# Decay and factors of the delta rule by way of DRAM, and another estimate behind the order of its instructions

## The chip, the cores and the metric

The kernel runs on one core of one Trainium2 chip. The metric is the time of one execution in microseconds (us); the median of three runs is 2485.27 us. The core's engines work side by side, each in the order of its own queue: PE (matmuls, with the weight load PEld in front of each), DVE and ACT (elementwise work), POOL (slow elementwise work, here also the inversion of small triangular matrices) and SP, which issues all DMAs. An instruction that waits holds up all that stand behind it in its queue.

## The reference

One step of a four-layer model on 576 positions (512 of a new stream, 64 of a running one), 1024 channels, fp32. The mixers are pool, delta rule, attention, pool; each is followed by a conv feed-forward block. The part that changes is the delta rule (layer 1, 8 heads of 128 channels):

```python
qkv = silu(causal_conv(h @ w_in)); q, k, v = split(qkv)      # q and k are normalised per head
gc = cumsum(g, axis=-1)                                       # log of the decay, within a chunk
decay = exp(where(lower_incl, gc[:,None] - gc[None,:], -inf))
sol = triangular_solve(eye + (k*beta) @ k.T * decay_strict, [v*beta, k*beta*exp(gc)])
attn = (q @ k.T) * decay
qg = q * exp(gc);  kg = k * exp(gc[-1] - gc);  glast = exp(gc[-1])
for c in chunks:                                              # the recurrence
    v_new = u_c - w_c @ s
    o_c = qg_c @ s + attn_c @ v_new
    s = s * glast_c + kg_c.T @ v_new
o = rmsnorm(o, norm_w) * silu(z);  y = o @ w_out
```

## The kernel before

All matrix products with weights are done as three passes of rounded high and low parts, so TensorE is the engine with the most work. The delta rule's stage (`dn`) begins with 32 projections of 48 matmuls each (8 heads each of k, q, v and z), issued in the order of a list (`TN['order']`), and ends with the output projection, 8 times 48 matmuls. Between the projections' matmuls stands the work of the heads:

- `conv` (k, q, v): DVE scales the projection out of PSUM into a tile C, POOL clears C's head and copies three old columns into it (`G.memset(C[:,0:3])`, `G.tensor_copy(C[:,515:518])`), ACT multiplies C by the last tap, POOL copies six columns of C out as new state (`dn_so`), DVE adds three taps, ACT takes tanh and writes it over C, DVE makes the silu. ACT's multiply thus waits for POOL's two set-up instructions, and its tanh for POOL's copies out of C.
- `mat(h)`: k times k (10 matmul passes on PE), decay and scale; the matrix M goes to DRAM.
- `inverse(g)` for four heads at once: POOL inverts 72 blocks of 32x32 in 62 tensor_tensor instructions; the result goes to DRAM. Other POOL work is queued in between.
- `merge(h)`: loads the blocks (16 DMAs), joins them to the inverse U of 128 rows.
- `prep_rec(h)`: attn, kg, q times exp(gc). For exp(gc) `bank(h, None, ...)` spreads the head's row gc over 128 partitions with two matmuls, and ACT takes the exponential out of PSUM in two instructions.
- `rec(h)`: the recurrence over five chunks. At its end 640 factors r (the rmsnorm) are made on POOL with a power. Five fp32 matmuls (ten passes) spread them over 128 partitions, and DVE multiplies o out of PSUM in two instructions. `z_post` multiplies with the gate, and ACT and DVE make the high and low parts that the output projection reads.

The order of the whole program is made when it is built. `Flow` holds a clock for each engine (`clk`), charges every instruction a duration from a table (`cost`), and lets the task of highest priority whose inputs are ready by those clocks write its next instructions; projections have the lowest priority and fill what is left. Each engine's queue is then fixed in the order written. In `Flow.charge` an instruction of DVE and one of POOL never hinder each other. Pools of tiles are limited by class: `lim['M']` = 2 and `lim['U']` = 2. For a DMA the estimate has the charges

```python
self.clk["S"] = max(self.clk["S"], t, self.now) + 475
self.clk["D"] = max(self.clk["D"], self.clk["S"] + 650) + size / 360.0
end = self.clk["D"] + 900
```

Of the kernel before, what the change touches and what calls it, by code (L numbers as in the profile page):

```python
# [9 lines left out]
F32 = mybir.dt.float32  # L10
F32R = mybir.dt.float32r
BF16 = mybir.dt.bfloat16
AF = mybir.ActivationFunctionType
ALU = mybir.AluOpType
PSUM = bass.MemoryType.PSUM
# [21 lines left out]
class Flow:  # L37
# [61 lines left out]
    def cost(self, eng, op, out, ins, a, k):  # L99
        n = self.cols(out)  # L100
        ps = any(x.space == PSUM for x in ins) or out.space == PSUM
        if eng == "PE":
            if op == "transpose":
                return 216.0
            rhs = a[2] if len(a) > 2 else k["rhs"]
            st = out.ap[0][0]
            base = out.offset // st if st else 0
            pair, self.half = (self.half == (base - 64, n) and out.shape[0] <= 64), (base, n) if out.shape[0] <= 64 else None
            if pair and rhs.dtype == F32:
                return 45.0  # L110
            if rhs.dtype == F32:
                return 4 * max(n, 128) / 2.4 + 6
            if rhs.dtype == F32R:
                return max(n, 256) / 2.4 + 3
            return max(n, 128) / 2.4 + 3
        if eng == "V":
            ptr = 62.0 * sum(1 for x in ins if self.cols(x) == 1 and n > 1)
            if op == "reciprocal":
                return 60 + 6.3 * n
            if op in ("tensor_copy", "tensor_scalar", "memset") and not ps:  # L120
                return 68 + 0.52 * n + ptr
            return 68 + 1.042 * n + ptr
        if eng == "A":
            return (51 if ps else 94) + 0.833 * n + 93 * sum(isinstance(k.get(q), bass.AP) for q in ("bias", "scale"))
        if eng == "G":
            if k.get("op") == ALU.pow:
                return 225 * n
            if op == "tensor_tensor":
                return 149 + 2.1 * n
            if op == "tensor_copy":  # L130
                return 118 + 3.3 * n
            return (36 if op == "memset" else 161) + 0.83 * n
        return 50.0
    def charge(self, eng, op, a, k):
        args = [x for x in list(a) + list(k.values()) if isinstance(x, bass.AP)]
        if not args:
# [4 lines left out]
        for x in ins:  # L141
            w = self.when(x, eng)
            if w < self.INF:
                t = max(t, w)
        n = out.tensor.name
        if eng == "S":
            size = max(self.cols(x) * x.shape[0] for x in (out, *ins)) * 4
# [3 lines that stand above are left out]
        else:  # L151
            if eng == "A":
                fn = str(k.get("func", a[2] if len(a) > 2 else "")).split(".")[-1]
                if fn in self.TABLES and fn not in self.aset:
                    self.aset = self.TABLES[fn]
                    t += 1283
            if eng != "PE":
                t = max(t, self.la[n] if not self.wr.get(n) else 0)
            end = t + self.cost(eng, op, out, ins, a, k)
            self.clk[eng] = end  # L160
        self.lastend = end
        self.lastcost = (end - t, op, self.cols(out), out.shape[0], str(out.dtype).split('.')[-1], ','.join('%s%s%s' % ('p' if x.space == PSUM else 's', self.cols(x), str(x.dtype).split('.')[-1]) for x in ins), 'p' if out.space == PSUM else 's')
        lo, hi = self.span(out)
# [90 lines left out]
 'prep': 10,  # L254
 'rec': 2,
 'cv': 6,
 'M': 2,
 'tu': 4,
 'tu_': 2,
 'mg': 3,  # L260
 'U': 2,
 'v': 2,
 'vs': 2,
 'pr': 4,
# [7 lines left out]
 'pv': 4,  # L272
 'pz': 6,
 'w': 8,
 'order': 'k0 q0 q1 k1 k2 q2 k3 q3 v2 v0 v1 v3 k4 q4 k5 k6 q6 k7 q5 q7 z1 z0 z2 z3 v5 v4 v6 v7 z4 z5 z7 z6',
 'pa': 3,
 'pb': 2,
 'pc': 7,
# [11 lines left out]
class Step:  # L290
# [354 lines left out]
    def ffn(self,l,st,nst,gnext):  # L645
# [55 lines left out]
        def up(j,stag):  # L701
            def gen():
                if j==0:
                    f.lim["g"]=6
                    yield [("so",1)]
                    so[0]=self.s([128,4,NF],F32,"so",1)
                f.spawn(post(j),10)
# [473 lines left out]
    def dn(self,l,st,nst,gnext):  # L1181
# [7 lines left out]
        cst=c1([128,3],"cst"); mc=c1([128,1],"mc")  # L1189
        tok=c1([128,5,72],"tok")  # L1190
        bE=c1([128,5,8],"bE"); ngc=c1([128,5,8],"ngc"); beta=c1([128,5,8],"beta"); nbe=c1([128,5,8],"nbe"); ekg=c1([128,5,8],"ekg")
        gh=[None]
        cc=[slice(128*c,128*c+128) for c in range(4)]; sm=slice(512,576); ss=slice(SO,SO+64)
        blocks=[(128*b,128*b+128) for b in range(4)]+[(512,576)]
        def prep():
# [15 lines left out]
        def ab_post(P):  # L1211
# [29 lines left out]
            G.memset(g[:,:NT].bitcast(F32),0.0)  # L1241
            V.tensor_copy(g[0:8,:NT],F[0:8])
            V.tensor_tensor(out=g[32:40,:NT],in0=F[0:8],in1=g[0:8,:NT].bitcast(F32),op=ALU.subtract)
            f.free(Yt,t_)
            yield [F,("p",1)]
            p=self.p()
# [32 lines left out]
        def first(post):  # L1279
            def gen():  # L1280
                f.lim["w"]=TN['w']
                yield [f"{st}:abw"]
                wk,hk=yield from self.wget()
                wa,ha=abw[0]
                Wp=((wk,[None,None],128),(wa,[None,None],40))
                for h in (0,1):
                    for w,P,n in Wp:
                        yield [("p",1,"g")]
                        P[h]=self.p("g")
                        yield from self.gemm(P,w,0,self.xk,KD,halves=(h,),need=self.xneed(st),n=n)  # L1290
                f.free(*hk,ha)
                f.spawn(ab_post(Wp[1][1]),3)
                f.spawn(post(Wp[0][1]),6)
            self.job(gen,(W[:,:,1024:1152],KD,128))
# [76 lines left out]

        def mat(h):
            k=kq[h][:,0]
            yield [k[:,:579],("a",1,"M"),("p",2),("t",1)]
            M=self.a(cls="M"); r=self.s([128,5],F32,"t",8)
            p=self.p(); q=self.p()
            G.memset(r,1.0)
            for c in range(4): mm(p[:,cc[c]],k[:,cc[c]],k[:,cc[c]],start=True,stop=True)
# [125 lines left out]
        def prep_rec(h):  # L1504
# [3 lines left out]
            yield [("a",2,"pr"),("a",1,"eg"),("p",2),("d",1,"ks"),("t",1)]  # L1508
            at=self.a(cls="pr"); eg=self.a(cls="eg"); kg=self.a(cls="pr"); kgs=self.d("ks")[:64]; gl=self.s([128,5],F32,"t",8)
            p=self.p(); q=self.p()  # L1510
            bank(h,self.mneg,p,q,0)
            yield [p,q,"@A"]
            for c in range(4): A.activation(at[:,cc[c]],p[:,cc[c]],AF.Exp,bias=ngc[:,c,h:h+1])
# [4 lines left out]
            yield [p,q,"@V"]  # L1518
            V.tensor_tensor(out=at[:,:512],in0=p,in1=at[:,:512],op=ALU.mult)
            V.tensor_tensor(out=at[:64,sm],in0=q[:64,:64],in1=at[:64,sm],op=ALU.mult)  # L1520
            yield [at]
            bank(h,None,p,q,0)
            yield [p,q,"@A"]
            A.activation(eg[:,:512],p,AF.Exp)
            A.activation(eg[:,sm],q[:,:64],AF.Exp)
            yield [eg]
            for b in range(4): T_(p[:,cc[b]],k[:,cc[b]],self.ident)
            T_(q[:64,:128],k[:,ss],self.ident)
            G.tensor_copy(gl[:,0:4],eg[:,127:512:128]); G.tensor_copy(gl[:,4:5],eg[:,575:576])
# [9 lines left out]
        def rec(h):  # L1539
# [56 lines left out]
            sq=self.a(cls="eg")  # L1596
            A.activation(sq[:,:NT],o[:,:NT],AF.Square)
            q=yield from sums(sq,512)
            f.free(sq)
            yield [("t",1)]  # L1600
            r=self.s([128,5],F32,"t",8)
            V.scalar_tensor_tensor(out=r,in0=q[:,:5],scalar=1.0/128,in1=eq[:,h],op0=ALU.mult,op1=ALU.add)
            G.tensor_tensor(out=r,in0=r,in1=mhalf,op=ALU.pow)
            yield [r,("p",1)]
            p=self.p()
            for i in range(4): mm(p[:,cc[i]],r[:,i:i+1].to_broadcast([128,128]),self.ident,start=True,stop=True)
# [8 lines left out]
        def z_post(h):  # L1615
# [25 lines left out]
                dno[h]=t  # L1641
                f.fire(f"{st}:o{h}")
            return g
        f.lim.update({k:TN[k] for k in ('cv','M','tu','tu_','mg','U','v','vs','pr','eg','ks','o_','S','rr')})
        def k_(h):
            if h: proj(8+h,qk_post(h,0),TN['pk'])
            else: first(qk_post(0,0))
# [390 lines left out]
```

## Time and profile before

| | us |
|---|---|
| median of three runs (2484.01 to 2489.79) | 2485.27 |
| the profiled execution | 2487.87 |
| its span, first to last instruction | 2486.1 |
| PE busy / PEld busy | 2440.4 / 2381.6 |
| DVE / ACT / POOL busy | 1904.6 / 1282.5 / 373.1 |
| mean granted TensorE clock, share of 2.4 GHz | 0.995 |

In the span the pool layer lies up to 145 us, its feed-forward block up to 435, the delta rule from 435 to 872, then feed-forward, attention (about 1436 to 1603), feed-forward, pool and the last feed-forward. All work of the helper `Eng.call` stands under one line of the code, L26, so that instructions are told apart by the tiles that they write and read: `p` is PSUM, `a` and `b` are wide SBUF tiles, `h` the split weights, `xh` and `xl` the parts of the normed input, `d` a small tile or a DRAM tensor, `t` the small tiles with the 640 factors.

### The profile page before, as it was taken

What the parts mean: (1) busy time and instruction counts of PE and PEld (TensorE: products, weight loads), DVE (VectorE), ACT (ScalarE), POOL (GpSimd) and SP (SyncE); (2) the same over time, 40 slices, a digit from 0 to 9 for tenths busy, and PEclk for the clock granted to TensorE, in tenths of its full rate; (3) what the DMA queues carried; (4) which work ended last, traced back from release to release, by engine and by line L of the source; (5) the groups of instructions that cost most, each with busy time, mean ns of one, the idle gap of its engine ahead of it and who ended that gap; (6) DMA issues with size and microseconds to landing.
All of it is one profiled execution on the core that took longest, in us unless ns stands there. A gap on an engine that the chain in (4) does not pass through costs nothing.

```text
span 2486.1 us, 46793 instructions
## 1 busy us (share of the span) xinstructions
PE 2440.4 (98%) x18385; PEld 2381.6 (96%) x18385; DVE 1904.6 (77%) x3695; ACT 1282.5 (52%) x2419; POOL 373.1 (15%) x750
## 2 busy tenths in 40 slices
PE   8999999998999999999999999999999999999998
PEld 7999999998999999999999998899999999999998
DVE  6888877887556478877886777778777788977775
ACT  6445544544344344444556677644444466544445
POOL 0000000138431101000000322200000011100000
PEclk9999999999999999999999999999999999999999
DMA  4323323332321221323334122222223231323231
GB/s 111 88 86 102 95 80 97 103 96 62 82 64 50 86 87 52 103 85 94 94 109 128 49 88 65 92 77 78 85 87 101 85 111 49 91 76 94 86 102 57
DMA packets 349056, 212.92 MB, mean 86 GB/s; under 512 B 30298, under 2 KB 341210, under 8 KB 348836
## 3 DMA queue, kind: packets, MB, share of 16 engines
q1 hardware_dynamic: 348836, 209.93, 28.9%
q8 instruction: 145, 2.38, 0.4%
q14 instruction: 75, 0.61, 0.1%
HBM read 192.41 MB, written 17.47 MB: 84 GB/s over the span
## 4 chain that ended last, share of the span: by engine, by line
PE 88%; DVE 4%; issue 3%; POOL 3%; DMA 1%; ACT 1%; SPq 0%; DVEq 0%; POOLq 0%; ACTq 0%
PE p L26 88%; DVE a L26 2%; DVE h L26 1%; POOL h L26 1%; POOL q L26 1%; ACT a L26 1%; DMA b<-in_x_prompt_dram 0%; DVE r L26 0%; DVE b L26 0%; POOL a L26 0%; DMA a<-in_cache_sb_k_dram 0%; ACT b L26 0%; POOL t L26 0%; POOL dn_so L26 0%; SPq L26 0%
## 5 line engine op out<-in xcount | busy, mean ns | idle before, releaser
L26 PE MATMUL p<-xh,h 128*128 128x288 f32 x4992 | 1061.5, 300 | 4.6 <-DVE h L26 4.4
L26 PEld LDWEIGHTS p<-xh,h 128*128 128x128 f32 x4992 | 820.9, 189 | 10.1 <-DVE h L26 4.8
L26 PE MATMUL p<-xl,h 128*128 128x288 f32 x2496 | 720.3, 296 | 0.0
L26 ACT ACTIVATE h<-r 128x512 fp32r<-128x512 f32 (+1 forms) x688 | 499.6, 747 | 411.6 <-PE p L26 327.3
L26 PE MATMUL p<-b,h 128*128 128x288 f32 x4992 | 677.9, 296 | 4.9 <-DVE b L26 2.3
L26 PEld LDWEIGHTS p<-b,h 128*128 128x128 f32 x4992 | 666.2, 189 | 8.1 <-DVE b L26 3.8
L26 DVE TENSOR_TENSOR h<-r,h 128x512 fp32r<-128x512 f32 (+1 forms) x688 | 571.5, 840 | 43.3 <-ACT h L26 41.8
L26 PEld LDWEIGHTS p<-xl,h 128*128 128x128 f32 x2496 | 472.8, 189 | 0.5
L26 DVE TENSOR_TENSOR a<-p,a 128x288 f32<-128x288 f32 (+4 forms) x662 | 269.5, 446 | 204.9 <-PE p L26 190.7
L26 PE MATMUL p<-a,h 128*128 128x288 f32 x2448 | 347.6, 295 | 4.6 <-DVE h L26 3.9
L26 PEld LDWEIGHTS p<-a,h 128*128 128x128 f32 x2448 | 331.8, 188 | 6.3 <-DVE h L26 4.8
L26 POOL COPY so<-a 128x2 f32<-128x2 f32 x176 | 98.1, 587 | 1488.6 <-DVE a L26 1488.6
L26 ACT ACTIVATE a<-a 128x512 f32<-128x512 f32 (+7 forms) x358 | 192.4, 559 | 130.6 <-DVE a L26 109.9
L26 ACT ACTIVATE q<-p 128x288 f32<-128x288 f32 x272 | 111.6, 410 | 168.4 <-PE p L26 165.0
L26 DVE SCALAR_TENSOR_TENSOR a<-a,fcw,a 128x578 f32<-128x578 f32 x176 | 144.2, 819 | 6.8 <-ACT a L26 1.7
L26 ACT ACTIVATE b<-a 128x576 fp32r<-128x576 f32 x96 | 65.4, 682 | 87.4 <-DVE a L26 87.3
L26 ACT ACTIVATE xh<-a,gains 128x288 fp32r<-128x288 f32 (+2 forms) x128 | 66.3, 531 | 70.2 <-DVE a L26 69.7
L26 DVE TENSOR_TENSOR a<-p,q 128x288 f32<-128x288 f32 (+2 forms) x204 | 66.6, 355 | 46.5 <-PE p L26 46.5
L26 ACT ACTIVATE a<-p 128x448 f32<-128x448 f32 (+5 forms) x149 | 64.8, 454 | 71.7 <-PE p L26 54.4
L26 POOL TENSOR_TENSOR a<-a,a 128x512 fp32r<-128x512 f32 (+1 forms) x64 | 68.2, 1065 | 220.7 <-DVE a L26 202.4
L26 DVE TENSOR_TENSOR r<-r 128x512 f32<-128x512 f32 x136 | 94.4, 694 | 4.1
L26 PE MATMUL p<-a,a 128*128 128x128 f32 (+6 forms) x656 | 94.4, 284 | 1.1 <-ACT b L26 0.8
(192 smaller groups left out, 2457.2 us busy)
## 6 DMA issues: line engine op xcount, KB each, us to landing
r<-in_ffn_w_up_dram SPq DMA_DIRECT2D x176, 512.0 KB
r<-in_ffn_w_down_dram SPq DMA_DIRECT2D x80, 512.0 KB
r<-in_dn_w_in_dram SPq DMA_DIRECT2D x32, 512.0 KB
r<-in_sb_w_qkv_dram SPq DMA_DIRECT2D x24, 512.0 KB
d<-a SPq DMA_DIRECT2D x24, 288.0 KB
a<-d SPq DMA_DIRECT2D x16, 288.0 KB
r<-in_ffn_w_down_dram SPq DMA_DIRECT2D x16, 256.0 KB
r<-in_dn_w_out_dram SPq DMA_DIRECT2D x8, 512.0 KB
```

The costliest lines, as they stand in the source:

```text
L26: r = f(*a, **k)
```

## The change

It has five parts, all within the delta rule's stage.

1. exp(gc): once per stage ACT takes the exponential of the 8 rows and SP writes them to DRAM (`eD`, 8x576). In `prep_rec` a DMA reads the head's row into all 128 partitions of `eg`; the two matmuls of `bank(h,None)` and the two exponentials out of PSUM are gone.
2. The factors r of heads 0 to 6: SP writes the 640 values to DRAM (a store of single elements), waits, reads them back into 128 partitions of `sq`; DVE multiplies in one instruction from SBUF. Head 7 keeps the matmuls. The tile `sq`, of class `eg`, is held until that multiply.
3. `Flow` gets a third clock, "port": while `turns` is on, an instruction of POOL that reads SBUF, and one of DVE that reads two wide SBUF operands (or is a copy or tensor_scalar from SBUF), begin only when the last such instruction has ended. `first` of the delta rule turns it on, the first up-projection of the next feed-forward block off. The instructions of attention stand in the same order as before, row by row.
4. `M` takes its tiles from class `U`, whose limit is 4.
5. The list of projections is another.

```diff
+    turns = False
+    def port(self, eng, op, ins):
+        n = sum(1 for x in ins if x.space != PSUM and self.cols(x) > 1)
+        if eng == "G":
+            return n > 0
+        return eng == "V" and (n > 1 or n == 1 == len(ins) and op in ("tensor_copy", "tensor_scalar"))
...
+            port = self.turns and self.port(eng, op, ins)
+            if port:
+                t = max(t, self.clk["port"])
             end = t + self.cost(eng, op, out, ins, a, k)
             self.clk[eng] = end
+            if port:
+                self.clk["port"] = end
...
- 'M': 2,
- 'U': 2,
+ 'U': 4,
...
- 'order': 'k0 q0 q1 k1 k2 q2 k3 q3 v2 v0 v1 v3 k4 q4 k5 k6 q6 k7 q5 q7 z1 z0 z2 z3 v5 v4 v6 v7 z4 z5 z7 z6',
+ 'order': 'k0 k1 q0 q1 k2 k3 q2 q3 v0 v1 k4 k5 q4 k6 k7 q5 q6 q7 v2 v3 z0 z1 v4 v5 z2 z3 v6 v7 z4 z5 z7 z6',
...
+            A.activation(t_[0:8,:NT],F[0:8],AF.Exp)
+            yield [t_[0:8,:NT]]
+            S.dma_start(out=eD,in_=t_[0:8,:NT])
...
-            M=self.a(cls="M"); r=self.s([128,5],F32,"t",8)
+            M=self.a(cls="U"); r=self.s([128,5],F32,"t",8)
...
+            S.dma_start(out=eg[:,:NT],in_=eD[h:h+1].to_broadcast([128,NT]))
             bank(h,self.mneg,p,q,0)
...
-            yield [at]
-            bank(h,None,p,q,0)
-            yield [p,q,"@A"]
-            A.activation(eg[:,:512],p,AF.Exp)
-            A.activation(eg[:,sm],q[:,:64],AF.Exp)
-            yield [eg]
+            yield [at,eg[:,:NT]]
...
+            if h<7:
+                f.free(q)
+                yield [r]
+                dr=self.dram([5,128])
+                with nc.allow_non_contiguous_dma(reason="640 factors"): S.dma_start(out=dr.rearrange("b p -> p b"),in_=r)
+                f.free(r)
+                yield [dr]
+                S.dma_start(out=sq[:,:NT],in_=dr.rearrange("(o b) p -> o (b p)",o=1)[:,:NT].to_broadcast([128,NT]))
+                yield [sq[:,:NT],"@V"]
+                V.scalar_tensor_tensor(out=o[:,:NT],in0=sq[:,:NT],scalar=nw,in1=o[:,:NT],op0=ALU.mult,op1=ALU.mult)
```

What moves in the queues shows at three places.

POOL, in the first inversion, where the set-up of the conv of k4 stands (a tile, 128x3: cleared, then three columns copied). `q<-h,h` and `h<-h,q` are the inversion's own instructions. Before:

```order
L26 TENSOR_TENSOR q_6626<-h_6621,h_6622 72x255
L26 TENSOR_TENSOR h_6622<-h_6622,q_6626 72x17x15
L26 TENSOR_TENSOR q_6626<-h_6621,h_6622 72x256
L26 TENSOR_TENSOR h_6622<-h_6622,q_6626 72x16x16
L26 MEMSET a_6964 128x3
L26 COPY a_6964<-dn_st 128x3
L26 TENSOR_TENSOR q_6626<-h_6621,h_6622 72x255
```

And after:

```order
L26 COPY dn_so<-a_6680 128x3 x2
L26 TENSOR_TENSOR q_6619<-h_6614,h_6615 72x175
L26 TENSOR_TENSOR h_6615<-h_6615,q_6619 72x25x7
L26 MEMSET a_6782 128x3
L26 COPY a_6782<-dn_st 128x3
L26 TENSOR_TENSOR q_6619<-h_6614,h_6615 72x192
L26 TENSOR_TENSOR h_6615<-h_6615,q_6619 72x24x8
```

The set-up of k4 stood behind 32 of the 62 instructions of the inversion and stands behind 14 now; that of k5 moves from 48 to 20, of k6 from 62 to 28, of k7 from 62 to 36.

SP, where the blocks for the merge of head 4 are loaded (`a<-d 32x4x32`, `32x32`, `64x4x64`). `r` is a weight tile. Before:

```order
L26 DMA r_8883<-in_dn_w_in_dram 128x8x128
L26 DMA out_dram<-d_8953 128x128
L26 DMA a_8956<-d_7402 32x4x32 x2
L26 DMA a_8956<-d_7402 32x32
L26 DMA a_8957<-d_8532 32x4x32 x4
L26 DMA a_8957<-d_8532 32x32 x2
```

And after:

```order
L26 DMA out_dram<-d_8826 128x128
L26 DMA d_8838<-t_8823 128x5x1
L26 DMA a_8804<-d_8838 128x576
L26 DMA a_8871<-d_129 128x576
L26 DMA a_8902<-d_7261 32x4x32 x2
L26 DMA a_8902<-d_7261 32x32
L26 DMA a_8903<-d_8582 32x4x32 x4
L26 DMA a_8903<-d_8582 32x32 x2
```

The store of a head's 640 factors, their read (which waits for the store to land) and the read of exp(gc) (`d_129`) for a later head now stand in front of the merge's loads.

PE, in the output projection after the spread of head 7's factors, up to its first matmul that reads head 7's result (`b_10269` before, `b_10202` after). Before:

```order
L26 MATMUL p_10254<-c_ident,t_10239 128x128 x4
L26 MATMUL p_10226<-c_ident,t_10239 128x64
L26 MATMUL p_10203<-b_10175,h_9796 128x288 x2
L26 MATMUL p_10204<-b_10175,h_9796 128x288 x2
L26 MATMUL p_10203<-b_10175,h_9797 128x288
L26 MATMUL p_10204<-b_10175,h_9797 128x288
L26 MATMUL p_10272<-c_ident,dn_so 72x128
L26 MATMUL p_10277<-c_ident,dn_so 72x128
L26 MATMUL p_10121<-b_10269,h_9427 128x288 x2
```

And after (the spread stands 24 matmuls above the first row):

```order
L26 MATMUL p_10211<-c_ident,dn_so 72x128
L26 MATMUL p_10167<-b_9950,h_9894 128x288 x2
L26 MATMUL p_10168<-b_9950,h_9894 128x288 x2
L26 MATMUL p_10167<-b_9950,h_9895 128x288
L26 MATMUL p_10168<-b_9950,h_9895 128x288
L26 MATMUL p_10222<-c_ident,dn_so 72x128
L26 MATMUL p_10167<-b_10147,h_9894 128x288 x2
L26 MATMUL p_10168<-b_10147,h_9894 128x288 x2
L26 MATMUL p_10167<-b_10147,h_9895 128x288
L26 MATMUL p_10168<-b_10147,h_9895 128x288
L26 MATMUL p_10092<-b_10202,h_9784 128x288 x2
```

Between the spread and head 7's first matmul stood 6 matmuls of the projection and two transposes; there are 36 and two now.

## Rows read from the trace of the kernel before

**Rows 1.** The page, busy us, share of the span and instructions of each engine.

```profile
PE 2440.4 (98%) x18385; PEld 2381.6 (96%) x18385; DVE 1904.6 (77%) x3695; ACT 1282.5 (52%) x2419; POOL 373.1 (15%) x750
```

**Rows 2.** Windows: start:end, length, busy of PE, PEld, DVE, ACT, POOL, clock, DMA.

```profile
145.00:440.00 295.00, 295.00 (x2220) 294.84 (x2220) 236.67 (x419) 148.97 (x270) 28.16 (x70) 1.00 0.33 96
440.00:690.00 250.00, 239.22 (x1815) 228.29 (x1815) 186.17 (x454) 111.99 (x234) 115.24 (x228) 0.99 0.31 83
```

**Rows 3.** PE in order of time: start, us, names, count, [idle before, its releaser].

```profile
539.10 0.40 PE L26 MATMUL p<-a,dn_idr 128*128 128x512 f32 x1
...
586.54 2.48 PE L26 MATMUL p<-b 128*128 128x128 f32 x10 [5.86 <-DVE b L26]
...
608.00 0.30 PE L26 MATMUL p<-a,dn_idr 128*128 128x64 f32 x1 [0.80 <-DVE a L26]
614.93 1.39 PE L26 MATMUL p<-b 128*128 128x128 f32 x10 [0.92 <-DVE b L26]
...
870.73 0.40 PE L26 MATMUL p<-b,h 128*128 128x288 f32 x1 [1.37 <-ACT b L26]
```

**Rows 4.** Windows again, the two stretches at the lower granted clock.

```profile
585.37:592.19 6.82, 5.65 (x25) 4.97 (x26) 4.88 (x19) 2.56 (x5) 6.30 (x13) 0.50 0.00 0
...
872.09:875.50 3.41, 3.41 (x16) 3.41 (x15) 2.83 (x7) 2.57 (x7) 0.00 (x0) 0.50 0.09 24
```

**Rows 5.** ACT and DVE in order of time: the convs of v3 and k4, others for comparison.

```profile
573.18 0.78 ACT L26 ACTIVATE a<-a,dn_cw 128x579 f32<-128x579 f32 x1 [5.30 <-POOL a L26]
...
585.01 0.69 ACT L26 ACTIVATE a<-a 128x579 f32<-128x579 f32 x1 [4.33 <-POOL dn_so L26]
...
547.24 2.54 DVE L26 SCALAR_TENSOR_TENSOR a<-a,dn_cw,a 128x579 f32<-128x579 f32 x3 [0.91 <-ACT a L26]
...
567.50 1.17 DVE L26 SCALAR_TENSOR_TENSOR a<-a,a 128x579 f32<-128x579 f32 x1
...
580.86 3.45 DVE L26 SCALAR_TENSOR_TENSOR a<-a,dn_cw,a 128x579 f32<-128x579 f32 x3
...
585.73 0.76 DVE L26 SCALAR_TENSOR_TENSOR b<-a,a 128x579 f32<-128x579 f32 x1 [1.41 <-ACT a L26]
```

**Rows 6.** PE in order of time: a spread of factors, a `bank(h,None)`, and what follows each.

```profile
667.37 1.33 PE L26 MATMUL p<-c_ident,t 128*128 128x128 f32 x10
668.53 0.67 PE L26 MATMUL p<-ones,a 128*128 128x1 f32 x5
...
714.56 0.50 PE L26 MATMUL p<-a,dn_idr 128*128 128x512 f32 x2
714.90 0.38 PE L26 MATMUL p<-xh,h 128*128 128x288 f32 x1
```

**Rows 7.** DVE's groups in the delta rule: names, shapes, count | busy, mean ns | idle.

```profile
L26 DVE SCALAR_TENSOR_TENSOR a<-a,a 128x576 f32<-128x576 f32 x8 | 6.5, 812 | 3.3 <-ACT a L26 3.3
...
L26 DVE SCALAR_TENSOR_TENSOR a<-p,dn_nw,a 128x512 f32<-128x512 f32 x8 | 6.0, 751 | 15.8 <-PE p L26 15.8
...
L26 DVE SCALAR_TENSOR_TENSOR a<-p,dn_nw,a 128x64 f32<-128x64 f32 x8 | 2.2, 275 | 0.0
```

**Rows 8.** SP, POOL and PE in order of time: DMA issues and who waited for one.

```profile
547.44 33.89 SPq L26 DMA_DIRECT2D r<-in_dn_w_in_dram  x5
...
607.19 0.25 POOL L26 TENSOR_TENSOR h<-h,q 72x31 f32<-72x31 f32 x1
...
610.50 11.10 SPq L26 DMA_DIRECT2D a<-d  x16
...
655.42 0.31 SPq L26 DMA_DIRECT2D h<-d  x1
...
658.92 0.25 POOL L26 TENSOR_TENSOR q<-h,h 72x31 f32<-72x31 f32 x1 [1.91 <-DMA h<-d]
...
671.84 0.54 SPq L26 DMA_DIRECT2D d<-in_state_dn_dram  x1
...
673.96 0.40 PE L26 MATMUL p<-d,b 128*64 128x128 f32 x2 [0.73 <-DMA d<-in_state_dn_dram]
```

More of the change, by code (lines that the diff above doesn't have):

```diff
@@ L704, in gen @@
                     f.lim["g"]=6
+                    f.turns=False
                     yield [("so",1)]
@@ L1191, in dn @@
         bE=c1([128,5,8],"bE"); ngc=c1([128,5,8],"ngc"); beta=c1([128,5,8],"beta"); nbe=c1([128,5,8],"nbe"); ekg=c1([128,5,8],"ekg")
-        gh=[None]
+        gh=[None]; eD=self.dram([8,NT])
         cc=[slice(128*c,128*c+128) for c in range(4)]; sm=slice(512,576); ss=slice(SO,SO+64)
@@ L1281, in gen @@
                 f.lim["w"]=TN['w']
+                f.turns=True
                 yield [f"{st}:abw"]
@@ L1373, in mat @@
             k=kq[h][:,0]
-            yield [k[:,:579],("a",1,"M"),("p",2),("t",1)]
-            M=self.a(cls="M"); r=self.s([128,5],F32,"t",8)
+            yield [k[:,:579],("a",1,"U"),("p",2),("t",1)]
+            M=self.a(cls="U"); r=self.s([128,5],F32,"t",8)
             p=self.p(); q=self.p()
@@ L1598, in rec @@
             q=yield from sums(sq,512)
-            f.free(sq)
             yield [("t",1)]
@@ L1603, in rec @@
             G.tensor_tensor(out=r,in0=r,in1=mhalf,op=ALU.pow)
+            if h<7:
[8 more added lines that the diff above has]
+                V.scalar_tensor_tensor(out=o[:,:NT],in0=sq[:,:NT],scalar=nw,in1=o[:,:NT],op0=ALU.mult,op1=ALU.mult)
+                f.free(sq)
+                oo[h]=o
+                f.fire(f"{st}:on{h}")
+                return
+            f.free(sq)
             yield [r,("p",1)]
@@ L1643, in z_post @@
             return g
-        f.lim.update({k:TN[k] for k in ('cv','M','tu','tu_','mg','U','v','vs','pr','eg','ks','o_','S','rr')})
+        f.lim.update({k:TN[k] for k in ('cv','tu','tu_','mg','U','v','vs','pr','eg','ks','o_','S','rr')})
         def k_(h):
```

## The prediction

> **What bounds the kernel now.** I read the busy times first: PE is busy 98% of the span and no other engine over 77% [rows 1]. So the time is that of PE's work, and of the places where PE is kept waiting or runs slower. The windows by stage [rows 2] tell where such places are: in the feed-forward block (145 to 440) PE is busy for all of 295 us, 2220 matmuls at 0.133 us each; in the delta rule's first 250 us (440 to 690) it is idle for 10.8. The change touches that stage alone, since in attention each engine's rows stand as before, so I price nothing there.
>
> The third view is PE in order of time [rows 3]. One wait makes up most of the idle time: 5.86 us at 586.54, for DVE's `b` of head 4's k (matmuls `p<-b`, k times k). Two more of the same kind follow at 608.00 (0.80) and 614.93 (0.92), and 1.37 us stand at the end, at 870.73, where the output projection waits for head 7. The clock windows [rows 4] show what came with the long wait: for 6.82 us the granted share was 0.50, that is 1.2 in place of 2.4 GHz, while PE worked for 5.65 us. PE had been idle just before. A second such stretch of 3.41 us follows the wait at the end.
>
> Why DVE was late shows on ACT and DVE [rows 5]. POOL is in its first inversion. ACT's multiply of v3 waited 5.30 us for POOL's set-up of its tile, which stood behind 26 instructions of the inversion; k4's three taps then began at 580.86 and took 3.45 us on DVE where the same three took 2.54 at 547.24, and its tanh waited again, for POOL's copy out of the tile. `b` came at 585.73. Nothing was wrong with PE's order except that it expected k4 some 6 us earlier. The old estimate lets DVE and POOL run side by side; the rows show that they lengthen each other (1.17 us at 567.50 for a form that took 0.76 at 585.73).
>
> **Part by part. Matmuls removed.** A spread of factors takes from 667.37 to 668.53, 1.16 us of PE [rows 6]; some others take 1.04, so I use 1.1. Seven of eight go: 7.7 us. A `bank(h,None)` takes from 714.56 to 714.90, 0.34 us [rows 6]; eight go: 2.7 us. Together **-10.4 us**. PE is busy at both places, so this is time of the path, unless a new wait takes it.
>
> **The new estimate and the list.** With the order of the change, the matmuls of k4 end 2.25 projections ahead of k times k of head 4, where they ended 1.12 ahead; for k5 it is 2.75 (1.0 before), for k6 2.5 (1.0), for k7 2.0 (0.9). A projection is 48 matmuls at 0.133 us, 6.4 us, so head 4 gets 14.4 us of cover in place of 7.2. It missed by 5.86. The cover is thus 1.3 us more than was needed at the slow pace of the row, and POOL's part of the delay falls too: k4's set-up stands behind 14 instructions of the inversion, not 32. For k5 the need was 6.4 + 0.92 us, the cover is 17.6. I take the waits at 586.54, 608.00 and 614.93 as gone: **-7.6 us**. With the long wait its stretch at half clock goes: 5.65 us of work at half pace lose 5.65/2, **-2.8 us** [rows 4].
>
> What is late next? The merges. PE reaches the first one 11.5 projections after M of head 3 has its mask, against 9.25 before: about 74 us of projections, some 14 of other work. The path by way of POOL is not longer: in the old trace that mask stood at 539.10 [rows 3], the inversion's last instruction at 607.19, the merges' loads began at 610.50, and the nine that the first product needs take 6 us at 11.10/16 each, and some 2 to land [rows 8]. So 80 us against 88: the inversion may become 8 us slower (DVE no longer stops for it) before PE feels it.
>
> **The end.** After the spread of head 7's factors, 36 matmuls and two transposes now stand ahead of the first that needs head 7; before it were 6 and two. 30 more matmuls are 4.0 us, and the wait was 1.37 us [rows 3]: **-1.4 us**. I don't count on the half-clock stretch behind it (3.41 us, 1.7 lost).
>
> **Transfers added.** 23: one store of exp(gc), eight reads of it, seven stores of factors, seven reads. On SP each costs about what others do, under 0.7 us (11.10 us for 16 [rows 8]), at most 16 us in over 200, and SP has time: it stood 33.89 us over five weight loads, waiting for free buffers [rows 8], so weights are far ahead. What matters is how long a reader waits. A small transfer took 2.1 us from issue to PE's first use (671.84 to 673.96), one of 288 KB took 3.5 us (655.42 to 658.92) [rows 8]. Exp(gc) is issued before the scores are masked and used after q times k; its trip lies beside them. The factors now need a store and a read, 2.1 + 3.5 = 5.6 us in place of one spread. But only z of the same head waits for them, and the next head's recurrence doesn't: I cost them at 0, hidden by other heads' chains and projections, for which PE has filler up to the end (the last head keeps its matmuls). Without that cover each of the 15 reads could cost up to 3.5 us; below nothing it can't be, since a transfer relieves nobody beyond the matmuls already counted.
>
> **DVE and ACT.** Per head 751 + 275 ns out of PSUM become one multiply of 128x576 from SBUF; the nearest row says 812 ns [rows 7]. ACT loses 16 exponentials and gains one. Both have slack, so 0. With POOL in an inversion a multiply with two SBUF operands took 1.17 us and another 0.76 [rows 5], so some of the seven will be longer. The Trainium skill, page "SBUF — State Buffer", section "Who interferes with whom", speaks against this part: by it a DVE instruction with two SBUF inputs blocks with a POOL instruction that reads SBUF, and one with a single SBUF input doesn't, so the old multiply out of PSUM was free of POOL and the new one isn't. By that rule, with those 0.41 us for each of seven and all of it on the path, the sum would be 2.9 us higher; by the rows DVE is idle for a quarter of the time from 440 to 690 [rows 2], and I add nothing.
>
> **Shared limit of M and U.** It moves order only; nothing to price.
>
> **New waits.** Towards the end the recurrences stand closer: the first begins at projection 20.25 of 32 in place of 18.4, with the same end, and in places a hundred small matmuls stand with hardly a projection among them. The old trace has small waits in such places, such as 0.73 us [rows 8]. I add **+2 us**, between 0 and 6.
>
> Sum: -10.4 - 7.6 - 2.8 - 1.4 + 2 = -20.2 us against the profiled execution's 2487.87. The median of the three runs is 2.6 us lower, 2485.27, so I forecast 2465.
>
> **Rivals.** (1) **The wait moves to the merges.** If DVE, no longer stopped, holds POOL up by more than those 8 us, PE waits for the first merge as long as it did for k4, with the same loss of clock. For it: the lengthened rows on DVE. Against it: the new estimate counts this very thing and puts the merge two projections later. Then only the matmuls are won: 2485.3 - 10.4 = 2475, within 2470 to 2480.
>
> (2) **SP's queue makes DVE late, and the kernel slower.** A head's store of factors, its read and the next read of exp(gc) stand directly in front of a merge's 16 loads, and the read waits on SP until the store has landed. DVE's multiply with exp(gc) holds up all of DVE behind it, evacuations of the recurrence too. If each of eight heads lost one trip of 3.5 us this way, 28 us would eat the 20: 2465 + 28 = 2493. It becomes slower by over 5 us (about 0.2%, what a measurement here can tell from no change) only from 3.2 us per head. Against it: SP's idle time and that PE has other heads' work. One page makes it likelier: the Trainium skill, "DMA: Bandwidth & Descriptors", section "Rules for kernel authors", says that a strided last dimension is moved as one descriptor per element, 640 here; no run here shows such a store, and by it the store alone could take longer than 2.1 us.
>
> (3) **Half of that**, 12 to 20 us of lateness: 2477 to 2488, around no change.
>
> **How the numbers follow.** Forecast 0.66 (2457 to 2471: all small waits and the second half-clock stretch gone at one end, six us of new waits at the other); rival 1 0.18; rival 3 0.09; rival 2 0.07. The range 2457 to 2479 takes in the forecast and most of rival 1. Faster by over 0.2%, below 2480.3: 0.66 + 0.18 + a part of rival 3, 0.86. Within 0.2%: 0.07. Slower: 0.07.
>
> **What would show it.** No wait of PE over 2 us between 540 and 640, no half-clock stretch there, `p<-c_ident,t` in ten passes instead of eighty, POOL's set-ups before DVE's taps. Wrong it would be if PE waits on `a<-d` or on a `p<-a,a` of the first merge (rival 1), or if DVE's idle time in front of the multiplies with `eg` or `sq` ends with a DMA and PE's idle time grows after 640 (rivals 2 and 3).

## The result and the profile after

The changed kernel takes 2524.61 us in the median (2522.30 to 2526.91) where the kernel before takes 2486.57 beside it: a ratio of 1.015, 95% interval 1.0137 to 1.0162. It is 38 us slower; the forecast was 2465, 20 us faster.

The busy times of the page after (as [rows 1]):

```profile
PE 2446.9 (97%) x18299; PEld 2389.2 (95%) x18299; DVE 1900.8 (75%) x3688; ACT 1278.0 (51%) x2404; POOL 378.8 (15%) x750
```

PE issues 86 matmuls fewer in the records and is busy 6.5 us longer: part of the work runs at the lower of the clock's two levels, as shown below. The windows of [rows 2], with the next one, after:

```profile
145.00:440.00 295.00, 293.96 (x2213) 293.75 (x2212) 237.42 (x420) 149.01 (x270) 28.16 (x70) 1.00 0.32 95
440.00:690.00 250.00, 244.64 (x1855) 234.00 (x1853) 184.79 (x456) 111.52 (x227) 124.45 (x236) 0.99 0.34 89
690.00:912.00 222.00, 181.94 (x1270) 170.32 (x1270) 92.49 (x185) 74.37 (x187) 32.58 (x70) 0.88 0.26 69
```

Up to 690 PE idles 5.4 us where it idled 10.8, about as forecast. From 690 on PE idles 40 of 222 us at a mean granted clock of 0.88 (before: 2.8 us at 0.99 in the same stretch). To compare kernels I use one window between two events that all have: ACT's table load near 459 us, inside the delta rule, and the next one, after its end. From the second of these to the last instruction it is 1570 to 1572 us in every kernel below but one (1574), and the part ahead of it differs by 3.6 us at most, so the differences lie inside. Before, then after:

```profile
459.63:915.44 455.81, 442.60 (x3374) 419.62 (x3373) 289.22 (x652) 196.14 (x439) 151.51 (x305) 0.99 0.28 76
```

```profile
461.01:954.25 493.24, 448.20 (x3288) 426.40 (x3287) 285.52 (x645) 192.25 (x424) 157.02 (x305) 0.94 0.30 79
```

37.4 us more: PE idles 45.0 instead of 13.2, and 86 matmuls fewer keep it busy 5.6 longer. PE in order of time (as [rows 3]), all its waits over 2 us:

```profile
609.65 2.48 PE L26 MATMUL p<-b 128*128 128x128 f32 x10 [2.34 <-DVE b L26]
...
695.64 0.76 PE L26 MATMUL p<-a,a 128*128 128x128 f32 x2 [3.61 <-DMA a<-d]
727.58 0.80 PE L26 MATMUL p<-d,a 128*128 128x128 f32 x2 [5.85 <-DVE d L26]
761.97 0.80 PE L26 MATMUL p<-d,a 128*128 128x128 f32 x2 [5.84 <-DVE d L26]
790.63 0.58 PE L26 MATMUL p<-d,a 128*128 128x128 f32 x1 [6.24 <-DVE d L26]
822.06 0.80 PE L26 MATMUL p<-d,b 128*128 128x128 f32 x2 [4.75 <-DVE d L26]
853.49 0.80 PE L26 MATMUL p<-d,a 128*128 128x128 f32 x2 [6.02 <-DVE d L26]
887.96 0.80 PE L26 MATMUL p<-d,a 128*128 128x128 f32 x2 [7.12 <-DVE d L26]
```

The wait of 5.86 us for head 4's k is gone: the four k times k of the second inversion stand at 576.12, 588.76, 602.01 and 609.65 now, and only the last of them, by the list head 7's, waits, 2.34 us. Six new ones wait for DVE's step of the recurrence (`d`), once per head. Follow the first one back, on SP and then on DVE:

```profile
711.71 0.37 SPq L26 DMA_DIRECT2D d<-t  x1
722.34 0.32 SPq L26 DMA_DIRECT2D a<-d  x1
```

```profile
718.56 0.89 DVE L26 TENSOR_TENSOR a<-p,a 128x288 f32<-128x288 f32 x3 [0.93 <-PE p L26]
726.45 0.82 DVE L26 SCALAR_TENSOR_TENSOR a<-a,dn_nw,a 128x576 f32<-128x576 f32 x1 [7.00 <-DMA a<-d]
727.18 0.35 DVE L26 SCALAR_TENSOR_TENSOR d<-p,dn_nbk,a 128x128 f32<-128x128 f32 x1
```

The store of a head's 640 factors (`d<-t`) is issued at 711.71. The read back waits on SP until the store has landed, 10.6 us. The multiply with the factors is next in DVE's queue and stands idle for 7.00 us; right behind it stands `d<-p,dn_nbk,a`, which PE needs for the next head's recurrence. DVE's waits, 640 to 900 us, in us, times, and the longest:

```profile
DVE a L26 <- DMA a<-d: 43.5, 7, 9.3
```

That is seven heads; the first waits 0.54 us, the six others 5.9 to 9.3.

What the store does in those 10.6 us shows in the DMA engines' packets, from its issue for 2 us and then up to the read's issue (711.71 to 713.71, 713.71 to 722.34):

```profile
DMA packets 656, 0.00 MB, mean 1 GB/s; under 512 B 656, under 2 KB 656, under 8 KB 656
```

```profile
DMA packets 0, 0.00 MB, mean 0 GB/s; under 512 B 0, under 2 KB 0, under 8 KB 0
```

All its packets have run 2 us after the issue. Then the trace has no packet of the core's 16 DMA engines for 8.6 us; the last completion event comes 10.5 us after the issue. So this store doesn't queue behind other transfers; the time passes between its last packet and its completion.

With each of PE's waits over 2 us comes a stretch at the lower of the two clock levels. The one at 609.65, and the first of the recurrences':

```profile
609.46:616.28 6.82, 6.63 (x27) 6.29 (x28) 6.30 (x21) 2.09 (x3) 5.90 (x13) 0.50 0.19 57
```

```profile
725.51:732.33 6.82, 4.75 (x21) 4.71 (x22) 5.70 (x11) 2.25 (x5) 0.00 (x0) 0.50 0.58 171
```

There are ten such stretches between 609 and 893 (two of them, at 746 and 807, behind no wait over 2 us), in which PE works 47.6 us in all; before there were two, 5.65 and 3.41 us of work [rows 4].

### The profile page after: what moved, and what is told of

It is laid out like the page before. It is cut to its first block, busy times and chain, and to the rows that moved or that the text cites. A ratio compares the mean times of both kernels' runs of the same rounds, so it can differ in the third digit from the quotient of the medians.

```text
span 2524.8 us, 46603 instructions
## 1 busy us (share of the span) xinstructions
PE 2446.9 (97%) x18299; PEld 2389.2 (95%) x18299; DVE 1900.8 (75%) x3688; ACT 1278.0 (51%) x2404; POOL 378.8 (15%) x750
## 4 chain that ended last, share of the span: by engine, by line
PE 85%; DVE 5%; issue 4%; DMA 4%; ACT 1%; POOL 1%; SPq 0%; DVEq 0%; POOLq 0%; ACTq 0%
PE p L26 85%; DVE a L26 3%; DMA d<-t 2%; DMA a<-d 1%; DVE h L26 1%; ACT a L26 1%; DMA b<-in_x_prompt_dram 0%; POOL t L26 0%; DVE r L26 0%; SPq L26 0%; DVE b L26 0%; POOL a L26 0%; DVE q L26 0%; DMA a<-in_cache_sb_k_dram 0%; ACT b L26 0%
## 5 line engine op out<-in xcount | busy, mean ns | idle before, releaser
L26 DVE TENSOR_TENSOR h<-r,h 128x512 fp32r<-128x512 f32 (+1 forms) x688 | 571.0, 839 | 42.6 <-ACT h L26 41.1
L26 DVE TENSOR_TENSOR a<-p,a 128x288 f32<-128x288 f32 (+5 forms) x662 | 269.1, 445 | 195.5 <-PE p L26 181.4
L26 ACT ACTIVATE a<-a 128x64 f32<-128x64 f32 (+7 forms) x359 | 193.2, 559 | 142.7 <-DVE a L26 135.2
L26 DVE TENSOR_TENSOR r<-r,r 128x512 f32<-128x512 f32 x136 | 93.5, 688 | 2.5
```

What stands on the lines that cost most here:

```text
L26: r = f(*a, **k)
```

## The experiments

Theory 1: the store of 640 single elements lands some 10 us after its issue, the estimate has about 2, and DVE and SP stand waiting for the rest. Theory 2: the new order packs the recurrences too closely. Theory 3: 23 more transfers are too many for SP's queue.

**e1_pe_factors**: the factors of all heads on PE again.

```diff
-            if h<7:
+            if h<0:
```

> The changed kernel with one part undone: the seven heads' factors are spread by PE again, as head 7's are; the new estimate, the list and exp(gc) by way of DRAM stay. Theory 1 (the store of 640 single elements takes about 10 us to land, the estimate has some 2, and DVE's multiply waits the rest): seven waits of DVE, 43.5 us in the changed kernel, go, with the PE waits of about 6 us and the half-clock stretches behind them; 7.7 us of matmuls come back, so 2465 + 8 = 2473, 2467 to 2480. Theory 2 (the new order packs the recurrences too closely, whatever the factors do): PE still waits some 6 us once per head, 2505 to 2530. Theory 3 (SP's queue is too long with 23 more transfers; now 9 more): part of the loss goes, 2480 to 2500.

Measured: 2476.68 us, ratio 0.9965 (0.9952 to 0.9978). No wait of PE over 2.4 us is left in the stage, and the window is

```profile
458.98:903.85 444.87, 436.93 (x3358) 415.96 (x3357) 286.72 (x652) 191.40 (x424) 156.55 (x305) 0.99 0.31 83
```

The whole loss hangs on the factors' trip. Theory 2 falls.

**e2_row_store**: as many transfers, but the factors are turned first, so that the store writes five rows of 512 bytes.

```diff
+                T_(q[:5,128:256],r,self.ident)
+                yield [q[:5,128:256]]
+                V.tensor_copy(sq[:5,:128],q[:5,128:256])
...
-                with nc.allow_non_contiguous_dma(reason="640 factors"): S.dma_start(out=dr.rearrange("b p -> p b"),in_=r)
+                S.dma_start(out=dr,in_=sq[:5,:128])
```

> The changed kernel, with the factors stored as five rows of 512 bytes: PE transposes them (one instruction), DVE copies 5x128 out of PSUM, SP stores that and reads it back in the same way. As many transfers as in the changed kernel, and the same rule of the estimate for them. Theory 1 (landing of single elements): the store lands in about 2 us, the read follows it on SP within 3 us, DVE's multiply waits under 2 us, and the time is 2460 to 2475. Theory 2 (order) and theory 3 (the number of transfers on SP): as the changed kernel, 2510 to 2530.

Measured: 2468.22 us, ratio 0.9926 (0.9911 to 0.9941), the fastest version here and faster than both kernels. SP, then DVE for the same head, then the window:

```profile
704.67 0.28 SPq L26 DMA_DIRECT2D d<-a  x1
705.91 0.32 SPq L26 DMA_DIRECT2D a<-d  x1
```

```profile
711.62 0.80 DVE L26 SCALAR_TENSOR_TENSOR a<-a,dn_nw,a 128x576 f32<-128x576 f32 x1
```

```profile
458.36:895.82 437.46, 431.15 (x3295) 409.94 (x3294) 286.54 (x652) 191.56 (x424) 157.58 (x305) 0.99 0.33 89
```

The same 2.5 KB landed in 1.2 us where they took 10.6 (1.2 to 3.9 in the seven heads); DVE doesn't wait here, and 2.9 us in all seven heads. Theory 3 falls, since the number of transfers is the same. Against this kernel the single elements cost 493.24 - 437.46 = 55.8 us: PE idle 45.0 against 6.3, 38.7 of it; and 17.1 us of longer work, though the changed kernel has seven matmuls fewer.

**e3_charged**: the same transfers, the estimate is told 8 us more.

```diff
-            end = self.clk["D"] + 900
+            end = self.clk["D"] + 900 + self.late
...
+                f.late=8000
                 with nc.allow_non_contiguous_dma(reason="640 factors"): S.dma_start(out=dr.rearrange("b p -> p b"),in_=r)
+                f.late=0
```

> The changed kernel; only the estimate is told that the store of single elements lands 8 us later than its rule has it. The same instructions in another order: the read is written behind other transfers on SP, the multiply behind other work on DVE. Theory 1: the trip of 10 us stays, but nobody in front waits for it: DVE's waits for a<-d in 640 to 900 fall from 43.5 us to under 10, and the time is 2460 to 2478. If the store itself is also in the way of other transfers, so that loads behind it land late, DVE's waits move to PE's for the merges and it stays above 2490. Theory 2 and 3: 2505 to 2530, as the same transfers and recurrences remain.

Measured: 2485.61 us, ratio 0.9996 (0.9986 to 1.0005). DVE's waits fall from 43.5 to 12.7 us, and 39 us of the loss with them, but 17 against e2 stay: my number was missed, and the sentence on transfers behind the store came true in mild form. SP, behind a store:

```profile
738.63 0.37 SPq L26 DMA_DIRECT2D d<-t  x1
739.47 0.35 SPq L26 DMA_DIRECT2D out_dram<-d  x1
739.87 15.44 SPq L26 DMA_DIRECT2D a<-d  x18
```

Four such groups behind a store take 12.6 to 15.4 us on SP. A merge's sixteen loads, with one or two more in places, take 7.6 to 11.9 us in before, e1 and e2, 21 of 24 groups under 10 ([rows 8] shows one of the long ones, 11.10). So the store seems to have a second price, for those who stand behind it; e9 below shows it with the order unchanged.

**e12_other_operand**: the changed kernel in the same order with all its transfers; DVE's multiply doesn't read what comes back.

```diff
-                V.scalar_tensor_tensor(out=o[:,:NT],in0=sq[:,:NT],scalar=nw,in1=o[:,:NT],op0=ALU.mult,op1=ALU.mult)
+                V.scalar_tensor_tensor(out=o[:,:NT],in0=o[:,:NT],scalar=nw,in1=o[:,:NT],op0=ALU.mult,op1=ALU.mult)
```

> The changed kernel, instruction for instruction in the same order, with all 23 transfers; only DVE's multiply of 128x576 reads o twice in place of the factors that came back (o times its weight times o: that part of the computation is another), so DVE no longer waits for the read. It separates the two prices of the store. If DVE's wait is all of the loss against e2_row_store (2468.2), the time is 2466 to 2472. If the transfers behind the store are late besides, as in e3_charged (2485.6) and e9_unread_640 (13.6 above before), 2478 to 2492, with PE waiting on loads. If DVE's wait only uncovers the next wait, above 2500.

Measured: 2487.38 us, ratio 0.9999 (0.9987 to 1.0010). One operand of seven instructions is worth 2524.6 - 2487.4 = 37 us: that is the price of DVE's wait, with the clock that follows. (The kernel before took 2486.6 beside the changed kernel and e2, 2488.2 beside e12, so that such differences are good to some 2 us.) Another 19 us against e2 (2487.4 - 2468.2) stay. Late loads are part of them:

```profile
678.99 0.38 SPq L26 DMA_DIRECT2D d<-t  x1
680.84 13.52 SPq L26 DMA_DIRECT2D a<-d  x18
```

```profile
690.95 0.79 PE L26 MATMUL p<-a,a 128*128 128x128 f32 x5 [2.96 <-DMA a<-d]
```

PE's waits for loads in e12's stage, us, times, and the longest (e2 has none):

```profile
PE p L26 <- DMA a<-d: 4.2, 2, 3.0
PE p L26 <- DMA d<-in_state_dn_dram: 4.2, 2, 2.4
```

The profiled execution of e12, one of its shortest (2482.16), is 14 us longer than e2's: 8.4 are these waits and 2.7 longer work in the window. The rest of the 14 is mostly other waits of PE, and the 5 us up to e12's median were not profiled.

**e5_factors_alone**: the branch `if h<7` of the change put into the kernel before, nothing else.

> The kernel before with the factors of seven heads by way of DRAM as single elements, and nothing else of the change: old estimate, old list. If the store's trip of about 10 us is enough to stop DVE in any order, seven waits of some 6 us as in the changed kernel, less 7.7 us of matmuls: 2505 to 2530. If it needs the denser recurrences of the new list, DVE waits little and the time is 2478 to 2495.

Measured: 2540.07 us, ratio 1.0211 (1.0196 to 1.0226), above the range I gave. DVE's waits for `a<-d` from 640 to 900 are 42.6 us in the old order as well. The new order isn't needed for the loss.

**e4_order_alone**: estimate, list and shared limit alone, no transfer added. **e7_no_turns**, **e8_old_list**: e1 with the old estimate, or with the old list.

```diff
-                f.turns=True
+                f.turns=False
```

> The kernel before with the new estimate, the list and the shared limit, and no transfer added: factors and exp(gc) are spread by PE. The order terms of the prediction (-7.6, -2.8, -1.4, +2) make -9.8 against before's 2486.6: 2477. Against e1_pe_factors (2476.7), which also has exp(gc) by way of DRAM: if those eight reads are hidden, this kernel is 2.7 us slower than it, about 2479; if they cost what their matmuls saved, the same 2476 to 2478; if the order gives nothing and e1's gain is exp(gc)'s alone, 2484 to 2488.

> e1_pe_factors with the old estimate (DVE and POOL don't take turns) and the new list. If the list alone removes the wait for head 4's k, the time is e1's, 2475 to 2478, with PE's gap near 608 no longer than 2.5 us; if the estimate has a part in it, an order in which POOL and DVE are taken as free of each other brings back waits of 3 us and more in the inversions, 2480 to 2488.

> e1_pe_factors with the list of before and the new estimate. If the estimate alone removes the wait for head 4's k, 2475 to 2478; if the list is what gives the cover (k4 two projections earlier), the wait of 5 to 6 us and its half-clock stretch stay: 2482 to 2487.

Measured: e4 2485.23, ratio 0.9998 (0.9989 to 1.0007); e7 2485.51, 0.9995 (0.9986 to 1.0005); e8 2490.35, 1.0012 (1.0003 to 1.0022). e7 fell as the estimate's share had it, e8 even above what the list's share gave. So neither the estimate nor the list gives anything clear of noise without the other, and e4 shows that both together without exp(gc) by DRAM don't either: e7 has waits of PE of 3.25 us at 570.05 and 4.66 at 602.19 for DVE's `b`, and e8 has

```profile
613.91 2.15 PE L26 MATMUL p<-ones,a 128*128 128x1 f32 x12 [6.39 <-ACT a L26]
```

e4 was expected at 2477 to 2479 and missed that. Its window, to be read beside e1's above:

```profile
458.81:910.70 451.89, 443.31 (x3374) 420.68 (x3373) 291.42 (x652) 196.20 (x438) 159.12 (x305) 0.99 0.29 76
```

PE's idle time is 8.6 us (13.2 before), so 4.6 are won; but PE is busy 0.7 us longer than before, not 2.8 shorter, as three short stretches of low clock (10.2 us in all) stand in for the old ones. e1 differs from e4 by exp(gc) alone, and its PE is busy 6.4 us less, with 2.7 us of matmuls fewer. The estimate writes another order as soon as a transfer replaces matmuls; of the other 3.7 us some 1.7 are clock (one stretch of 6.8 us in e1 against 10.2, half of it lost), the rest is open. So e1's 10 us can't be shared out between the order and exp(gc).

**What of the store takes the time.** Seven kernels add a store that nobody reads to the kernel before; the factors still go over PE. e9_unread_640 has the 640 elements of the change:

```diff
+            if h<7:
+                yield [r]
+                dr=self.dram([5,128])
+                with nc.allow_non_contiguous_dma(reason="640 factors"): S.dma_start(out=dr.rearrange("b p -> p b"),in_=r)
```

The others differ in one thing: e6_store_unread (1 to 5 columns of 128), e10_unread_128 (`dr` is [128,5], `out=dr`), e11_unread_act (`A.dma_start`), e13_unread_128x4 (one column), e14_apart_128x4 (one column, `dr` is [128,128], `out=dr[:,0:1]`), e15_apart_640x4 (all five, `dr` is [640,128], only its first column written).

> The kernel before with a store of factors that nobody reads: for heads 0 to 6 1, 2, 3, 4, 5, 5, 5 columns of 128 single elements. Theory 1: the time from issue to landing grows with the number of elements, from about 2 us for 128 to 8 to 10 us for 640, with no PE wait of its own; the kernel stays within 2482 to 2494. Rival: the landing is as short as a small transfer's, about 2 us, for all of them; then the 9.5 to 10.6 us between store and read in the changed kernel are queueing behind other transfers.

> The kernel before with a store of 640 single elements for each of heads 0 to 6 that nobody reads; the factors are still spread by PE. No engine waits for its landing. If the store costs only those who wait for it, the time is before's, 2484 to 2490. If it also holds up the transfers behind it (e3_charged: 16 to 18 loads issued behind a store took 12.6 to 15.4 us on SP where they take 8 to 9 elsewhere), PE waits for merge loads or states: 2492 to 2505.

> As e9_unread_640 in the same order, the same 2560 bytes to 128 pieces of 20 bytes instead of 640 of 4 (the array in DRAM has the partition as its first dimension). If the number of pieces is what takes the time, the store lands in a fraction of the 640 elements' 9 to 10 us, about 3 us, and the kernel takes before's time, 2484 to 2490. If it is any write from 128 partitions of small pieces, both take the same.

> As e9_unread_640 in the same order, the store of 640 single elements issued by ACT instead of SP. If the loads are late because they stand behind the store in SP's own queue, their delay goes, and the time is 2484 to 2490, plus what ACT's issue costs; if the store keeps the DMA engines themselves busy, the loads are as late as in e9, within 3 us of its time.

> As e9_unread_640, but each of the seven unread stores writes only 128 single elements side by side in DRAM (512 bytes in all). If the number of pieces sets the time, they land like e10_unread_128's 128 pieces of 20 bytes, in 1.4 to 4.1 us, and the kernel takes 2484 to 2490; if writing pieces of 4 bytes is slow in itself, they land in some 7 us, as head 0's in e6_store_unread, and the time is 2487 to 2500.

> As e13_unread_128x4, with the 128 elements 512 bytes apart in DRAM. If neighbouring small pieces get in each other's way, these land in 1.4 to 4.1 us while e13's take some 7; if small pieces are slow in themselves, both take the same.

> As e9_unread_640, with the 640 elements 512 bytes apart in DRAM. If neighbours are the cause, they land in under 5 us and the kernel takes 2484 to 2490; if it is the number or the size of the pieces, 9 to 11 us and 2495 to 2505 as in e9.

"Lands" is the last of the store's completion events that the trace has, counted from its issue.

| kernel | pieces | lands after, us | us | ratio (95%) |
|---|---|---|---|---|
| e6 | 128 to 640 of 4 bytes, side by side | 7.2, 8.3, 8.8, 9.5, then 8.7 to 10.8 | 2497.19 (one run) | |
| e9 | 640 of 4 bytes, side by side | 8.5 to 11.0 | 2500.36 | 1.0056 (1.0041 to 1.0071) |
| e13 | 128 of 4 bytes, side by side | 7.2 to 8.8 | 2493.53 | 1.0026 (1.0014 to 1.0037) |
| e10 | 128 of 20 bytes, side by side | 1.4 to 4.3 | 2486.16 | 0.9999 (0.9990 to 1.0009) |
| e14 | 128 of 4 bytes, 512 bytes apart | 1.4 to 4.2 | 2487.36 | 1.0001 (0.9989 to 1.0012) |
| e15 | 640 of 4 bytes, 512 bytes apart | 2.0 to 4.4 | 2487.94 | 1.0002 (0.9991 to 1.0013) |
| e11 | as e9, issued by ACT | 8.7 to 11.1 | 2532.70 | 1.0188 (1.0171 to 1.0205) |

e6 missed on both counts: the first store was slow already, and 2497 is above the 2494 I allowed. Nobody waits for e9's store, and yet it costs 14 us. SP and PE of e9 at the sixth head, and SP of e15 and of before at the same place:

```profile
822.76 0.36 SPq L26 DMA_DIRECT2D d<-t  x1
823.22 0.46 SPq L26 DMA_DIRECT2D d<-in_state_dn_dram  x1
823.78 12.94 SPq L26 DMA_DIRECT2D a<-d  x16
```

```profile
832.17 0.69 PE L26 MATMUL p<-d,b 128*64 128x128 f32 x2 [3.69 <-DMA d<-in_state_dn_dram]
```

```profile
815.69 0.36 SPq L26 DMA_DIRECT2D d<-t  x1
816.15 0.46 SPq L26 DMA_DIRECT2D d<-in_state_dn_dram  x1
816.71 7.67 SPq L26 DMA_DIRECT2D a<-d  x16
```

```profile
816.42 7.63 SPq L26 DMA_DIRECT2D a<-d  x16
```

In e9 the load of the head's state, issued right behind the store, comes so late that PE waits 3.69 us (three such waits take 7.0 us in e9, one takes 0.7 before). The sixteen loads take 12.94 us on SP where before has 7.63; in e13 they take 10.83, in e10 and e14 7.66. In e15 they take 7.67 us, as without a store. I had expected the number of pieces to be the cause; e10 alone would have seemed to prove it. e13 and e15 tell otherwise: 128 pieces of 4 bytes side by side are slow, 640 pieces far apart are not. What is slow is single elements of 4 bytes that neighbour each other in DRAM; at 20 bytes neighbours do no harm. Sizes between 4 and 20 bytes and distances between 4 and 512 were not tried, so the limit stays open.

e11 takes the store out of SP's queue, and it gets worse, by 32 us against e9. ACT issues it shortly ahead of a merge's loads or among them. Four of six such groups of sixteen loads then take 12.9 to 15.3 us on SP, and PE waits for them up to 7.43 us; the two groups in which the store came 3.5 us before their end took 8.0 and 8.5. So a store in ACT's queue holds up loads in SP's: the delay isn't a matter of one issuing queue's order alone. The Trainium skill, "DMA: Bandwidth & Descriptors", section "Issuing engines are not separate DMA queues", says that transfers issued by different engines run on the same DMA engines and interleave; the four slow groups agree. Whether the part that both queues share here is the DMA engines or the memory behind them, the traces don't tell. How much of the 32 us is the earlier start and how much the other queue wasn't separated.

## Why the prediction was wrong, point by point

- **What bounds the kernel; matmuls removed.** Right. In e2, where the store is harmless, 2468.2 stands beside the forecast's 2465, inside the forecast's own range (2457 to 2471), and the window is 18.4 us shorter than before, where the sum said 20.2. (The forecast's upper end, from six us of new waits, should have been 2469.) The terms inside don't all agree: PE's idle time fell by 6.9 us, where the waits with the end and the new ones made 7.0, but its busy time by 11.5, where the matmuls and the clock made 13.2. e2 also has seven transposes on PE that the sum doesn't have, and the clock's term didn't come, as the next point says; that the total is so near is in part luck.
- **The new estimate and the list** (-7.6 and -2.8). The three waits near 586, 608 and 615 are gone in the changed kernel and in e1, as forecast; the one at 608.00 was not of the same kind, though, since its row waits for `a`, not for a k. But a wait of 2.34 us for the last k came instead, with 0.75 and 1.10 elsewhere, so the forecast's sign "no wait of PE over 2 us between 540 and 640, no half-clock stretch there" failed. The size was too large by about a third: PE's idle time fell from 13.2 to 7.9 us in e1, 5.3, where the waits with the end (-1.4) and the new ones (+2) made 7.0. The clock's term failed: with that shorter wait the stretch at half clock stayed, 6.63 us of work in e1 and in the changed kernel, and e2 has three of 3.41 us, where before had 5.65 and 3.41. And e4, which has the order alone, is at 0.9998 of before (0.9989 to 1.0007), where the four terms (-7.6, -2.8, -1.4, +2) made -9.8 us.
- **The end.** Right: no wait over 0.7 us stands in front of the output projection in e1 and e2.
- **Transfers added, costed at 0.** This is the step that failed, in three places. First, the bound: "a small transfer took 2.1 us from issue to PE's first use", and I took that row, a load of 64 KB, for the store of factors. The read, at 3.5, was sized right (722.34 to DVE's start at 726.45, 4.1 us); the store took 10.6 where the bound was 2.1. Second, "only z of the same head waits for them": the multiply stands in DVE's queue in front of the next head's recurrence, so everybody waited; e12 prices that at 37 us. Third, no price was set on transfers behind the store: 19 us against e2 stay in e12, of which its trace shows 8.4 as PE's waits for loads, and the unread stores of e9 cost 14.
- **Rival 2** had the mechanism (SP's read waits for the store, DVE's multiply holds up the recurrence) and the right sign, with a chance of 0.07 and 3.5 us per head: 28 us for eight heads, where 55.8 for seven were measured against e2, 8.0 each. Its price lacked the store's landing, the half-clock stretch behind every wait of PE, and the late loads. The sentence on the Trainium skill's rule ("DMA: Bandwidth & Descriptors", section "Rules for kernel authors": one descriptor per element for a strided last dimension) pointed at this store, and a store that no row of before shows should have had a wide upper bound. The trace agrees with the rule (656 packets for 640 elements). But the count is not what costs: e15 writes just as many single elements with no loss.
- **The multiply from SBUF** (weighed with the Trainium skill, "SBUF — State Buffer", section "Who interferes with whom"). Adding nothing was right: the seven multiplies took 0.80 to 0.82 us in the changed kernel and in e2, as the row of 812 ns said [rows 7]. The case that the Trainium skill speaks of hardly came up: in the changed kernel the second inversion ends at 715.69, and only the first multiply (704.02) lies in it.
- **Exp(gc) by DRAM**, its reads at 0: no run shows a loss by them. e1 has these reads and is 8.6 us faster than e4, which has the matmuls; 2.7 were forecast, but the orders differ too, so this is not the price of the matmuls.
- **What would show it wrong** named the main loss: DVE's idle time in front of the multiplies with `sq` ending with a DMA, and PE's idle time growing after 640.

## To carry to other kernels

Before a few values are sent through DRAM, look how the store's pieces lie there: single 4-byte elements side by side landed in 7 to 11 us and held up the loads behind them, whole rows in 1.2 to 3.9, and one small transpose on PE with a copy on DVE bought that. A transfer that stands between two engines is priced by its slowest leg and by what is queued behind the instruction that waits for it, on DVE as on SP; where the trace of before has no such transfer, a small kernel that adds it unread measures it. And an order that comes from an estimate is only as good as the estimate's price for a new kind of instruction: with 8 us more on that store the same transfers cost 39 us less.

## What the runs showed of the hardware that I had not expected

- 640 elements of 4 bytes 512 bytes apart land in 2.0 to 4.4 us, 128 of them side by side in 7.2 to 8.8 (e15, e13). In the changed kernel the packets of such a store have all run 2 us after its issue, and the trace then has no packet for 8.6 us, up to the read that waits for the landing. The reason behind that can't be seen in these traces.
- Such a store slows transfers issued after it: at one place of the same order sixteen loads took 12.94 us (e9) and 10.83 (e13) instead of 7.6 to 7.7 (before, e10, e14, e15). A store issued on ACT's queue does it to loads on SP's (e11).
- From e13 to e9, five times as many pieces take only some 2 us longer to land; the kernel's loss grows from 6.0 to 13.6 us.
